# A fourth PSUM bank for the Gram products of a hybrid decoder layer, the upper rows of each inverse loaded first, and new orders for the last block and the drain

## The chip, the cores and the metric

The kernel runs on one core of one Trainium2 chip. The metric is the device time of one execution in microseconds (us); the figure for a kernel is the median of several executions. The engines are TensorE (PE in the profile; its weight loads are PEld), VectorE (DVE), ScalarE (ACT), GpSimd (POOL) and SyncE (SP, which here only issues DMAs). SBUF is the on-chip working memory, PSUM the eight banks into which TensorE writes.

## The reference, cut to what matters

One decoder layer on a sequence of 2048 tokens and a width of 1024. The part that the change touches is the RWKV-7 recurrence, which the kernel computes in chunks of 64 tokens, and the first steps of the SSD mixer behind it.

```python
def _rwkv7_scan(r, w, k, v, za, zb):          # 8 heads of 64
    def step(S, inp):
        r_t, w_t, k_t, v_t, a_t, b_t = inp
        sa = jnp.einsum("bhij,bhj->bhi", S, a_t)
        S = S * w_t[:, :, None, :] + sa[..., None] * b_t[:, :, None, :] + v_t[..., None] * k_t[:, :, None, :]
        return S, jnp.einsum("bhij,bhj->bhi", S, r_t)
    ...
def reference(x, ...):                          # DEPTH = 1
    xn = _rms_norm(h, pre_mix_norm[l])
    proj = (xn @ w_in[l]).astype(jnp.float32)
    p_ssd, p_rwkv = jnp.split(proj, [SSD_COLS], axis=-1)
    y_ssd = _ssd_mixer(p_ssd, ...)              # conv, softplus steps, chunked SSD, gate, norm
    y_rwkv = _rwkv7_mixer(p_rwkv, ...)          # token shift, low-rank decay, _rwkv7_scan, group norm, gate
    mix = jnp.concatenate([y_ssd, y_rwkv], axis=-1).astype(h.dtype) @ w_out[l]
    h = h + _rms_norm(mix, post_mix_norm[l])
    hn = _rms_norm(h, pre_ffn_norm[l])
    u = _causal_dwconv(hn @ ffn_w_up[l], ffn_conv_w[l], ffn_conv_b[l])
    gate, val = jnp.split(u, 2, axis=-1)
    f = (jax.nn.silu(gate) * val) @ ffn_w_down[l]
    h = h + _rms_norm(f, post_ffn_norm[l])
```

## The kernel before, in words

The program has three phases. The recurrence phase (`phase_R`, up to about 1005 us) works on 16 blocks of 128 tokens, two chunks of 64 each; `phase_S` does the SSD mixer and the output projection; `phase_F` the gated feed-forward part, which takes the second half of the span. Matrix products in float16 are done as three passes (high by high, high by low, low by high).

In the recurrence phase the order of TensorE's work is written out by hand: an iteration `it` runs through a list of step names, in which `f.` is block `it` (its front half), `b.` block `it - 1` (its back half), `a.` block `it - 2`, and `n.load` fetches the rows of block `it + 1`. FIRST is the list of iteration 0, SECOND of iteration 1, PLAN of iterations 2 to 14, LAST of iteration 15. DRAIN has only back steps; each `S` in it takes one step of the list S_DRAIN, the first work of the SSD phase. Only TensorE keeps the order of the lists. From iteration 1 on the order on VectorE, ScalarE, GpSimd and in SyncE's DMA queue is made at build time by a scheduler, which simulates the program and lets each engine take the instruction that is ready, earlier ones of the program first; each engine then keeps that order on the chip.

The front half of a block: `d.0` to `d.13` are projections of 24 matmuls each (L301), evicted in pairs by ScalarE (L439, L441) and mixed with the previous token by VectorE (L443); `low` is the low-rank decay, `scan` its running sum (L508) and two exponentials (L512, L513), `keys` and `norm` the normalised key (a square on ScalarE, L519, then the matmul `nq`, L527, a logarithm and an exponential, then BK on GpSimd and VectorE, L541 and L542). `conv.0` to `conv.7` are the projections of the SSD branch, with a causal convolution of taps (L464 on GpSimd, L469 and L474 on VectorE, stored by L475). `gram.0` and `gram.1` multiply BK with AR, per chunk and half of the heads one PSUM bank (`gr00`, `gr01`, `gr10`, `gr11`, L558), which VectorE masks into G (L562).

`solve` inverts the 64x64 triangular parts of G as 32x32 halves: SyncE writes them to DRAM (L574, two DMAs for each chunk) and reads them back one matrix per partition (`atl`, L578); a chain of 31 steps, each a product and a sum (L593, L596), does the substitution, on VectorE in every block but the last and on GpSimd there; the inverses go to DRAM (L601) and back into the tile XT (L607, four DMAs: for chunk `c` and half `b`, with `b` the inner loop). In the next iteration `merge.0` first transposes the upper half's inverse (XW, L641, one instruction on VectorE for each chunk, each of which needs the half `b = 0` of its chunk), then multiplies (`pw`, L648); `merge.1` (`po`, L652) completes the inverse. `own`, `update` and `state` are the products with the state of the recurrence, for chunk 0 and then chunk 1; `gate` and `finish` give the block's output (`finish.0` ends on GpSimd, L740; `finish.1` begins with transposes `yt` on TensorE, L745).

PSUM: the tag `ms` has 3 banks in rotation, used by `gr`, `nq`, `bt`, `vt`, `bo` and the low-rank products; `mm` has 2; `B` (merges, gate, `yt`), `U` and `Q` have one each. Eight are in use.

Of the kernel before, what the change touches and what calls it, by code (L numbers as in the profile page):

```python
# [209 lines left out]
f.chain.6 f.taps.5 f.chain.7 f.conv.7.0 f.taps.7  # L210
"""
SECOND = """
f.d.0 b.values f.d.1 f.d.2 f.d.3 f.d.4 f.low.0 b.own.0 f.low.1 f.scan f.d.5 f.keys f.d.6 f.d.7 f.d.8 b.merge.0 f.d.9
f.conv.0 f.conv.1 f.norm f.conv.2 f.conv.3 b.merge.1 f.receptance f.conv.4 b.update.0 f.gram.0 f.conv.5 f.gram.1
f.d.10 f.conv.6 f.conv.7 b.state.0 b.own.1 f.d.11 b.update.1 f.transposed.0 b.gate f.solve f.transposed.1 f.d.12
b.state.1 b.finish.0 f.d.13 n.load
"""
PLAN = """
f.d.0 f.d.1 b.values f.low.0 f.d.2 a.finish.1 f.d.3 f.d.4 f.low.1 f.scan f.d.5 f.d.6 f.d.7 b.own.0 f.d.8 f.conv.0 f.keys
f.d.9 f.conv.1 b.merge.0 f.norm f.conv.2 b.merge.1 f.conv.3 b.update.0 f.conv.4 f.receptance f.gram.0 f.gram.1 f.solve  # L220
n.load f.conv.5 f.conv.6 b.state.0 f.conv.7 b.own.1 f.transposed.0 f.d.10 f.d.11 b.update.1 f.d.12 b.state.1 b.gate
f.transposed.1 f.d.13 b.finish.0
"""
LAST = """
f.d.0 f.d.1 f.low.0 f.d.2 f.d.3 a.finish.1 f.d.4 f.d.5 f.low.1 f.scan b.values f.keys f.d.6 f.d.7 f.d.8 f.d.9 f.norm b.own.0
f.d.10 f.receptance f.d.11 b.merge.0 f.d.12 f.gram.0 b.merge.1 f.d.13 f.gram.1 f.solve b.update.0 f.conv.0 b.state.0
f.conv.1 b.own.1 f.conv.2 f.conv.3 b.update.1 f.transposed.0 f.conv.4 f.conv.5 b.state.1 f.transposed.1 f.conv.6
b.gate f.conv.7 b.finish.0
"""
DRAIN = """  # L230
S S b.values S S a.finish.1 S b.own.0 S S S S S S S S S S S S S S S S b.merge.0 S b.merge.1 S b.update.0 S b.state.0 S
b.own.1 S S b.update.1 S b.state.1 b.gate S b.finish.0 b.finish.1
"""


# [70 lines left out]
def phase_R(tc, K, const, tables, x, w_r, w_c, wl_d, g2_d, XN, XC, YR, filler, iters=16):  # L306
    nc = tc.nc
    V, S, G_ = nc.vector, nc.scalar, nc.gpsimd
    with ExitStack() as ctx:
# [56 lines left out]
        ub0 = (64, 0)  # L366
# [17 lines left out]
        def bank(name, tag, bufs=1):  # L384
            return psp.tile([P, 4, P], F32, name=name, tag=tag, bufs=bufs)

        class Block:
# [164 lines left out]
                        out=tr[:, j], in0=tr[:, j], scalar=K.p_r_k[:, j:j + 1], in1=tk[:, j], op0=ALU.mult, op1=ALU.mult)  # L552

            def gram(self, c):
                pg = [self.ms(f"gr{c}{hh}") for hh in range(2)]
                for j in range(4):
                    for hh in range(2):
                        nc.tensor.matmul(  # L558
                            pg[hh][:, j, :], self.BK[64 * hh:64 * hh + 64, j, c, :], self.AR[64 * hh:64 * hh + 64, j, c, :],
                            start=True, stop=True)  # L560
                for hh in range(2):
                    V.tensor_tensor(  # L562
                        out=self.G[:, c, hh], in0=pg[hh],
                        in1=K.gmask[:, c * P:(c + 1) * P].unsqueeze(1).to_broadcast([P, 4, P]), op=ALU.mult)
# [23 lines left out]
            def chain(self, part):  # L588
                atl, xl, tmp, XTd, it = self.atl, self.xl, self.tmp, self.XTd, self.it
                chain = G_ if it == iters - 1 else V  # L590
                for j in range(part * 4, min(part * 4 + 4, 31)):
                    n, m = 31 - j, j // 4 + 1
                    chain.tensor_tensor(  # L593
                        out=tmp[:, :m, :n], in0=atl[:, j, j + 1:32].unsqueeze(1).to_broadcast([P, m, n]),
                        in1=xl[:, :m, j:j + 1].to_broadcast([P, m, n]), op=ALU.mult)
                    chain.tensor_tensor(  # L596
                        out=xl[:, :m, j + 1:32], in0=xl[:, :m, j + 1:32], in1=tmp[:, :m, :n], op=ALU.add)
                if part < 7:
                    return
# [21 lines left out]
            def values(self):  # L621
# [148 lines left out]
        for it in range(iters + 1):  # L770
            if it == 1:
                begun.close()
            f = blocks[it] if it < iters else None
            b = blocks[it - 1] if it else None
# [10 lines left out]
            for step in (FIRST if b is None else SECOND if it == 1 else DRAIN if f is None else LAST if it == iters - 1 else PLAN).split():  # L785
# [10 lines left out]
                a = [int(v) for v in a]  # L796
# [1136 lines left out]
```

## Time and profile before

| | |
|---|---|
| median of 3 executions | 2626.78 us (2623.9 to 2636.14) |
| the profiled execution | 2628.14 us, of which the span from first to last instruction is 2626.4 us |
| TensorE busy | 2439.2 us, 93% of the span |
| VectorE, ScalarE, GpSimd busy | 75%, 46%, 50% |
| mean granted TensorE clock | 0.977 of full speed |
| iterations 2 to 14 | 173 to 874 us |
| iteration 15 (LAST) | 874 to 938 us |
| drain, to the last transposes | 938 to 1005 us |

All numbers of the trace are from this one profiled execution; times in it count from its first instruction. Columns and forms are explained with each group of rows.

### The profile page before, as it was taken

How to read it: one execution, taken by the hardware profiler on the slowest of the kernel's cores; microseconds unless marked ns; L12 is line 12 of the kernel's file. 1: busy time of each engine (PE TensorE's matmuls, PEld its weight loads, DVE VectorE, ACT ScalarE, POOL GpSimd, SP SyncE). 2: the span in 40 equal slices, each digit the busy share in tenths (PEclk: the TensorE clock that was granted, in tenths of full speed). 3: DMA queues.
4: the chain of work that ended last, by engine and by line, in shares of the span. 5: the costliest groups of instructions: out<-in, count | busy, mean ns of one | idle time of the engine just before them, and what ended most of it. 6: DMA issues, size and time to landing. Idle time of an engine off the chain costs nothing. (4 is left out here: it accounts for less than half of the span.)

```text
span 2626.4 us, 53869 instructions
## 1 busy us (share of the span) xinstructions
PE 2439.2 (93%) x21196; PEld 1536.1 (58%) x21212; DVE 1970.8 (75%) x3687; ACT 1211.5 (46%) x2467; POOL 1301.0 (50%) x1356
## 2 busy tenths in 40 slices
PE   5889999999999888999987999999989999999998
PEld 4788888888888855555543444444434444444443
DVE  6778777777877756677787979999999836455557
ACT  7455555555555444444544553534444433223132
POOL 2344444544444353445577675866757513223035
PEclk8899999999999999999998999999999999999999
DMA  7332222232222243556575444444436543333253
GB/s 219 72 70 67 54 61 57 64 86 54 54 64 56 48 170 121 158 162 177 154 209 184 167 147 154 142 171 168 149 128 204 168 143 102 103 96 106 87 156 109
DMA packets 344414, 319.14 MB, mean 122 GB/s; under 512 B 203232, under 2 KB 248672, under 8 KB 340832
## 3 DMA queue, kind: packets, MB, share of 16 engines
q1 hardware_dynamic: 342864, 314.12, 40.9%
q8 instruction: 166, 2.72, 0.5%
q10 hardware_dynamic: 1296, 1.58, 0.2%
q14 instruction: 88, 0.72, 0.1%
HBM read 187.85 MB, written 110.99 MB: 114 GB/s over the span
## 5 line engine op out<-in xcount | busy, mean ns | idle before, releaser
L1399 PE MATMUL u<-b,w 128*128 128x512 f16 x3696 | 811.2, 382 | 28.5 <-DVE C L1417 11.2
L1399 PEld LDWEIGHTS <-w 128*128 128x128 f16 x3696 | 363.1, 98 | 473.6 <-issue 38.8
L301 PE MATMUL d<-xt,wr 128*128 128x129 f16 x5376 | 337.8, 225 | 19.1 <-DMA xt<-xh 15.4
L301 PEld LDWEIGHTS <-wr 128*128 128x128 f16 x5376 | 323.2, 100 | 33.3 <-ACT wr L264 15.4
L1635 PE MATMUL d<-dw,fa 128*128 128x512 f16 x1512 | 333.7, 380 | 4.6 <-DVE dw L1599 2.3
L1635 PEld LDWEIGHTS <-fa 128*128 128x128 f16 x1596 | 157.1, 98 | 205.5 <-issue 19.1
L1417 DVE TENSOR_TENSOR C<-u,C 128x512 f32<-128x512 f32 x220 | 150.5, 684 | 156.3 <-PE u L1399 151.0
L301 PE MATMUL c<-xt,wc 128*128 128x131 f16 x3072 | 203.2, 225 | 18.7 <-ACT tr L441 9.6
L301 PEld LDWEIGHTS <-wc 128*128 128x128 f16 x3072 | 186.5, 99 | 35.3 <-issue 27.6
L1648 DVE TENSOR_TENSOR acc<-d,acc 128x512 f32<-128x512 f32 x212 | 140.1, 683 | 54.3 <-PE d L1635 53.4
L593 DVE TENSOR_TENSOR tmp<-atl,xl 128x60 f32<-128x60 f32 (+24 forms) x465 | 140.6, 302 | 41.5 <-DMA atl<-ATd 30.1
L1245 POOL TENSOR_TENSOR fa<-p,fa 128x512 f16<-128x512 f32 x100 | 142.1, 1434 | 40.1 <-ACT fa L1240 40.1
L1247 DVE SCALAR_TENSOR_TENSOR w<-us,w 128x512 f16<-128x512 f32 x132 | 144.5, 1105 | 17.4 <-ACT w L1240 16.4
L1452 DVE SCALAR_TENSOR_TENSOR p<-C,fpar,p 128x1024 f32<-128x1024 f32 x88 | 131.1, 1490 | 33.9 <-ACT p L1448 33.7
L469 DVE SCALAR_TENSOR_TENSOR ca<-rc,cw,ca 128x128 f32<-128x128 f32 x384 | 130.3, 385 | 24.8 <-POOL ca L464 24.5
L596 DVE TENSOR_TENSOR xl<-xl,tmp 128x60 f32<-128x60 f32 (+24 forms) x465 | 124.0, 267 | 11.3
L1452 DVE SCALAR_TENSOR_TENSOR a<-C,fpar,a 128x1024 f32<-128x1024 f32 x88 | 123.5, 1404 | 4.8 <-ACT a L1448 3.5
L1240 ACT ACTIVATE fa<-p 128x512 f16<-128x512 f32 x110 | 65.5, 623 | 131.9 <-DVE p L1465 120.0
L1371 POOL TENSOR_TENSOR us<-us,us 128x512 f32<-128x512 f32 x66 | 104.5, 1587 | 43.9 <-DVE w L1247 25.2
L706 POOL TENSOR_TENSOR tS<-S,Pi 64x256 f32<-64x256 f32 x64 | 41.4, 647 | 163.6 <-DVE S L716 161.2
L1458 POOL COPY fcarry<-C 128x2 f32<-128x2 f32 x88 | 40.5, 461 | 164.7 <-DVE C L1417 164.7
L1413 ACT ACTIVATE C<-u 128x512 f32<-128x512 f32 x88 | 52.0, 591 | 148.2 <-PE u L1399 128.5
(316 smaller groups left out, 4571.0 us busy)
## 6 DMA issues: line engine op xcount, KB each, us to landing
UW<-w SPq DMA_DIRECT2D x154, 256.0 KB
w<-UW SPq DMA_DIRECT2D x154, 256.0 KB
us<-in_w_u_dram SPq DMA_DIRECT2D x88, 256.0 KB
DW<-dw SPq DMA_DIRECT2D x70, 256.0 KB
dw<-DW SPq DMA_DIRECT2D x56, 256.0 KB
hs<-HN SPq DMA_DIRECT2D x48, 256.0 KB
r<-in_w_d_dram SPq DMA_DIRECT2D x10, 1024.0 KB
xin<-in_x_dram SPq DMA_DIRECT2D x16, 512.0 KB
```

Source lines behind the costliest of these rows:

```text
L301: nc.tensor.matmul(ps, w[:, a, kt, :], xt[:, b, kt, cols], start=n == 0, stop=n == 3 * KT - 1)
L469: V.scalar_tensor_tensor(out=acc[:, q], in0=raw[:, q, k:k + 128], scalar=cw[:, g + q, k:k + 1], in1=acc[:, q], op0=ALU.mult, op1=ALU.add)
L593: chain.tensor_tensor(out=tmp[:, :m, :n], in0=atl[:, j, j + 1:32].unsqueeze(1).to_broadcast([P, m, n]), in1=xl[:, :m, j:j + 1].to_broadcas ...
L596: chain.tensor_tensor(out=xl[:, :m, j + 1:32], in0=xl[:, :m, j + 1:32], in1=tmp[:, :m, :n], op=ALU.add)
L1245: {"V": V, "G": G_}[engine].tensor_tensor(out=l, in0=src, in1=h, op=ALU.subtract)
L1247: V.scalar_tensor_tensor(out=l, in0=src, scalar=scale, in1=h, op0=ALU.mult, op1=ALU.subtract)
L1371: op("G", 1.25, lambda: G_.tensor_tensor(out=st[o], in0=st[a], in1=st[b], op=alu), (n[a], n[b]), (n[o],))
L1399: nc.tensor.matmul(bk[at], self.w[i][:, u, k, :], self.half.b[i][:, k, v, :], start=start and n == 0, stop=n == 11, skip_group_check=True)
L1417: op("V", .61, lambda: V.tensor_tensor(out=part(j, x), in0=bk[at], in1=part(*a), op=ALU.add), (("u", 4 * s + at), (*(c0, c1)[a[0]], a[1])) ...
L1452: V.scalar_tensor_tensor(out=o[j], in0=C[j][:, 2 - d:1026 - d], scalar=cw[:, g, 2 - d:3 - d], in1=o[j], op0=ALU.mult, op1=ALU.add)
L1635: nc.tensor.matmul(bk[s, t], pairs[m].a[i][:, u, t * P:t * P + P], pairs[m].w[n][0][:, v, :], start=new and m == 0 and u == v == 0, stop=m ...
L1648: V.tensor_tensor(out=acc[j][:, t], in0=bk[s, t], in1=acc[j][:, t], op=ALU.add)
```

## The change

The Gram products of the second chunk's second half (`gr11`) get the bank of tag `B` in iterations 2 to 14 instead of one of `ms`. The four loads of XT run over `b` outside and `c` inside. The two transposes at the head of `merge.0` become a step of their own, `turn`, which every list has directly before `merge.0`. LAST, DRAIN and S_DRAIN are reordered: in LAST `low` and `norm` come earlier among the `d` steps, `own.0` comes behind `merge.0`, `gram.1` and `solve` stand around `d.13`; in DRAIN `own.0` comes earlier, `a.finish.1` later, `finish.0` ahead of two S steps; in S_DRAIN `t.steps` and `s.flip` come earlier, `c.keys` later.

```diff
 S_DRAIN = """
-s.steps c.z.0 c.z.1 c.z.2 c.z.3 s.sums n.z.0 s.flip c.rows n.z.1 n.z.2 n.z.3 c.begin m.z.0 c.off c.keys c.decay.0 m.z.1
-c.decay.1 m.z.2 m.z.3 t.steps u.z.0 u.z.1 u.z.2 n.rows c.y u.z.3 c.state
+s.steps c.z.0 c.z.1 c.z.2 c.z.3 s.sums s.flip n.z.0 c.rows n.z.1 n.z.2 n.z.3 c.begin m.z.0 t.steps c.off c.decay.0
+m.z.1 m.z.2 m.z.3 c.decay.1 u.z.0 c.keys u.z.1 n.rows c.y u.z.2 c.state u.z.3
 """
...
 LAST = """
-f.d.0 f.d.1 f.low.0 f.d.2 f.d.3 a.finish.1 f.d.4 f.d.5 f.low.1 f.scan b.values f.keys f.d.6 f.d.7 f.d.8 f.d.9 f.norm b.own.0
-f.d.10 f.receptance f.d.11 b.merge.0 f.d.12 f.gram.0 b.merge.1 f.d.13 f.gram.1 f.solve b.update.0 f.conv.0 b.state.0
-f.conv.1 b.own.1 f.conv.2 f.conv.3 b.update.1 f.transposed.0 f.conv.4 f.conv.5 b.state.1 f.transposed.1 f.conv.6
-b.gate f.conv.7 b.finish.0
+f.d.0 f.d.1 f.d.2 f.d.3 f.d.4 f.low.0 f.low.1 f.d.5 a.finish.1 f.scan b.values f.keys f.d.6 f.norm f.d.7 f.d.8 f.d.9
+f.receptance f.d.10 b.turn b.merge.0 f.d.11 b.own.0 f.gram.0 b.merge.1 f.d.12 f.gram.1 f.d.13 f.solve f.conv.0 b.update.0
+b.state.0 f.conv.1 b.own.1 f.conv.2 b.update.1 f.conv.3 b.state.1 f.conv.4 f.transposed.0 f.conv.5 f.conv.6
+f.transposed.1 b.gate f.conv.7 b.finish.0
 """
 DRAIN = """
-S S b.values S S a.finish.1 S b.own.0 S S S S S S S S S S S S S S S S b.merge.0 S b.merge.1 S b.update.0 S b.state.0 S
-b.own.1 S S b.update.1 S b.state.1 b.gate S b.finish.0 b.finish.1
+S S b.values b.own.0 S S S S S S S a.finish.1 S S S S S S S S S S S S b.turn b.merge.0 S b.merge.1 b.update.0 S
+b.state.0 S b.own.1 S S b.update.1 S b.state.1 b.gate b.finish.0 S S b.finish.1
 """
...
             def gram(self, c):
-                pg = [self.ms(f"gr{c}{hh}") for hh in range(2)]
+                side = c == 1 and 1 < self.it < iters - 1
+                pg = [self.ms(f"gr{c}0"), bank("gr11" + self.sf, "B") if side else self.ms(f"gr{c}1")]
...
-                for c in range(2):
-                    for b in range(2):
+                for b in range(2):
+                    for c in range(2):
                         r0 = ub0[c] + 32 * b
                         K.marks["solved"] = nc.sync.dma_start(
                             XT[r0:r0 + 32, :, 32 * b:32 * b + 32], XTd[c, b].rearrange("h x q i -> (x q) h i"))
...
+            def turn(self):
+                self.X11 = self.tl("XW", (8, 32))
+                for c in range(2):
+                    b0 = ub0[c]
+                    V.transpose(self.X11[b0:b0 + 32], self.XT[b0:b0 + 32, :, 0:32])
+
             def merge(self, step):
 
                 XT, Gv = self.XT, self.Gv
-                if step == 0:
-                    self.X11 = self.tl("XW", (8, 32))
-                    for c in range(2):
-                        b0 = ub0[c]
-                        V.transpose(self.X11[b0:b0 + 32], XT[b0:b0 + 32, :, 0:32])
                 X11 = Wm = self.X11
```

## Rows read from the trace of the kernel before

**Rows 1.** The page's part 1: engine, busy us, share, instructions.

```profile
PE 2439.2 (93%) x21196; PEld 1536.1 (58%) x21212; DVE 1970.8 (75%) x3687; ACT 1211.5 (46%) x2467; POOL 1301.0 (50%) x1356
```

**Rows 2.** TensorE's waits in iterations 2 to 14: waiter, releaser, total us, times, longest.

```profile
PE gr L558 <- DVE G L562: 17.8, 13, 1.4
PE pw L648 <- DVE XW L641: 9.1, 14, 1.9
```

**Rows 3.** TensorE's timeline, one turn: start, us, instruction, [idle before, releaser].

```profile
564.51 0.69 PE L648 MATMUL pw<-XW,G 32*32 32x32 f32 x30 [0.34 <-DVE XW L641]
...
572.58 1.38 PE L558 MATMUL gr<-AR,BK 64*128 64x128 f32 x18 [0.22 <-DVE BK L542]
575.41 1.16 PE L558 MATMUL gr<-AR,BK 64*128 64x128 f32 x14 [1.44 <-DVE G L562]
...
619.79 0.69 PE L648 MATMUL pw<-XW,G 32*32 32x32 f32 x30 [0.53 <-DVE XW L641]
```

**Rows 4.** VectorE's timeline in the same turn.

```profile
575.92 0.43 DVE L474 SCALAR_TENSOR_TENSOR ca<-ct,ca 128x256 f32<-128x256 f32 x1
576.39 1.29 DVE L562 TENSOR_TENSOR G<-gr,cst 128x512 f32<-128x512 f32 x2
...
586.44 0.19 DVE L593 TENSOR_TENSOR tmp<-atl,xl 128x31 f32<-128x31 f32 x1 [1.42 <-DMA atl<-ATd]
...
611.47 0.17 DVE L596 TENSOR_TENSOR xl<-xl,tmp 128x8 f32<-128x8 f32 x1
...
619.30 0.43 DVE L641 STREAM_TRANSPOSE XW<-XT 32x256 f32<-32x256 f32 x1 [0.34 <-DMA XT<-XTd]
```

**Rows 5.** SyncE's queue in that turn: start and us of the issues, line, DMA, count.

```profile
561.38 1.83 SPq L607 DMA_DIRECT2D XT<-XTd  x4
...
576.39 0.40 SPq L475 DMA_DIRECT2D XC<-ca  x1
...
577.41 1.28 SPq L411 DMA_TRANSPOSE xt<-xh  x1
578.79 1.03 SPq L574 DMA_DIRECT2D ATd<-G  x2
```

**Rows 6.** VectorE's waits for XT, iterations 2 to 14, and the longest, in its timeline.

```profile
DVE XW L641 <- DMA XT<-XTd: 24.1, 20, 2.5
...
508.53 0.43 DVE L641 STREAM_TRANSPOSE XW<-XT 32x256 f32<-32x256 f32 x1 [2.11 <-DMA XT<-XTd]
```

**Rows 7.** Iteration 15: TensorE and VectorE around `nq`; two other turns' scan and its input.

```profile
887.39 5.68 PE L301 MATMUL d<-xt,wr 128*128 128x129 f16 x96
898.64 2.08 PE L527 MATMUL nq<-sq,cst 128*128 128x512 f32 x2 [5.57 <-ACT sq L519]
...
890.71 0.47 DVE L596 TENSOR_TENSOR xl<-xl,tmp 128x8 f32<-128x8 f32 x1
...
892.07 2.17 DVE L508 TENSOR_TENSOR_SCAN Pv<-smask,thw 128x512 f32<-128x512 bf16 x1 [0.17 <-POOL thw L507]
...
556.75 1.22 DVE L508 TENSOR_TENSOR_SCAN Pv<-smask,thw 128x512 f32<-128x512 bf16 x1
...
606.72 1.50 POOL L507 TENSOR_SCALAR thw<-thw 128x512 f32<-128x512 f32 x1
```

**Rows 8.** A stretch behind `nq`: us, busy us (instructions) of PE, PEld, DVE, ACT, POOL, clock, DMA, GB/s.

```profile
898.60:908.60 10.00, 9.96 (x90) 8.18 (x90) 6.66 (x14) 3.97 (x7) 2.97 (x2) 0.57 0.16 41
```

**Rows 9.** TensorE's longest waits in the drain.

```profile
PE yt L745 <- POOL ysb L740: 5.7, 1, 5.7
PE z L957 <- DVE ws L265: 4.0, 2, 3.6
PE acs L922 <- DVE da L917: 2.2, 1, 2.2
```

**Rows 10.** The drain: GpSimd's work of `finish` inside the chain, and TensorE's `u.z.3`.

```profile
952.70 1.33 POOL L750 TENSOR_TENSOR yln<-yln,tv 128x512 f32<-128x512 f32 x1
...
992.92 1.47 PE L957 MATMUL z<-ws,xs 128*128 128x512 f16 x6
```

More of the change, by code (lines that the diff above doesn't have):

```diff
@@ L212 @@
 SECOND = """
-f.d.0 b.values f.d.1 f.d.2 f.d.3 f.d.4 f.low.0 b.own.0 f.low.1 f.scan f.d.5 f.keys f.d.6 f.d.7 f.d.8 b.merge.0 f.d.9
-f.conv.0 f.conv.1 f.norm f.conv.2 f.conv.3 b.merge.1 f.receptance f.conv.4 b.update.0 f.gram.0 f.conv.5 f.gram.1
+f.d.0 b.values f.d.1 f.d.2 f.d.3 f.d.4 f.low.0 b.own.0 f.low.1 f.scan f.d.5 f.keys f.d.6 f.d.7 f.d.8 b.turn b.merge.0
+f.d.9 f.conv.0 f.conv.1 f.norm f.conv.2 f.conv.3 b.merge.1 f.receptance f.conv.4 b.update.0 f.gram.0 f.conv.5 f.gram.1
 f.d.10 f.conv.6 f.conv.7 b.state.0 b.own.1 f.d.11 b.update.1 f.transposed.0 b.gate f.solve f.transposed.1 f.d.12
@@ L218 @@
 PLAN = """
[L219 to L222, printed above, removed]
+f.d.0 f.d.1 b.values f.low.0 f.d.2 a.finish.1 f.d.3 f.d.4 f.low.1 f.scan f.d.5 f.d.6 f.d.7 b.own.0 f.d.8 f.conv.0
+f.keys f.d.9 f.conv.1 b.turn b.merge.0 f.norm f.conv.2 b.merge.1 f.conv.3 b.update.0 f.conv.4 f.receptance f.gram.0
+f.gram.1 f.solve n.load f.conv.5 f.conv.6 b.state.0 f.conv.7 b.own.1 f.transposed.0 f.d.10 f.d.11 b.update.1 f.d.12
+b.state.1 b.gate f.transposed.1 f.d.13 b.finish.0
 """
 LAST = """
-f.d.0 f.d.1 f.low.0 f.d.2 f.d.3 a.finish.1 f.d.4 f.d.5 f.low.1 f.scan b.values f.keys f.d.6 f.d.7 f.d.8 f.d.9 f.norm b.own.0
-f.d.10 f.receptance f.d.11 b.merge.0 f.d.12 f.gram.0 b.merge.1 f.d.13 f.gram.1 f.solve b.update.0 f.conv.0 b.state.0
-f.conv.1 b.own.1 f.conv.2 f.conv.3 b.update.1 f.transposed.0 f.conv.4 f.conv.5 b.state.1 f.transposed.1 f.conv.6
-b.gate f.conv.7 b.finish.0
+f.d.0 f.d.1 f.d.2 f.d.3 f.d.4 f.low.0 f.low.1 f.d.5 a.finish.1 f.scan b.values f.keys f.d.6 f.norm f.d.7 f.d.8 f.d.9
+f.receptance f.d.10 b.turn b.merge.0 f.d.11 b.own.0 f.gram.0 b.merge.1 f.d.12 f.gram.1 f.d.13 f.solve f.conv.0 b.update.0
+b.state.0 f.conv.1 b.own.1 f.conv.2 b.update.1 f.conv.3 b.state.1 f.conv.4 f.transposed.0 f.conv.5 f.conv.6
+f.transposed.1 b.gate f.conv.7 b.finish.0
 """
 DRAIN = """
-S S b.values S S a.finish.1 S b.own.0 S S S S S S S S S S S S S S S S b.merge.0 S b.merge.1 S b.update.0 S b.state.0 S
-b.own.1 S S b.update.1 S b.state.1 b.gate S b.finish.0 b.finish.1
+S S b.values b.own.0 S S S S S S S a.finish.1 S S S S S S S S S S S S b.turn b.merge.0 S b.merge.1 b.update.0 S
+b.state.0 S b.own.1 S S b.update.1 S b.state.1 b.gate b.finish.0 S S b.finish.1
 """
```

## The prediction

> **What bounds the kernel now.** I read the busy shares first: TensorE is the fullest engine by far [rows 1], which suggests that every wait of TensorE that goes is time gained. Then TensorE's waits by releaser in iterations 2 to 14: the largest entry is the one that the fourth bank removes, 13 waits of `gr11` for the eviction of `gr00`, 17.8 us; beside it stand 14 waits for the transposed inverse XW, 9.1 us, at most 1.9 [rows 2]. So TensorE is nearly full, and yet it waits in nearly every iteration for the solve of the block before. To see which of the two sets the pace I followed one turn through the timelines of three engines, from one `merge.0` to the next [rows 3 to 5]. It takes 619.79 - 564.51 = 55.28 us: from `pw` to the first `gr` 8.07 (`nq` is queued right behind `pw`, and `gr` again waits a little, 0.22, for BK, which comes from `nq`); from there to the end of the second eviction pair, 576.39 + 1.29 = 577.68, 5.10; to the chain's first step 8.76, through SyncE's DMAs, with VectorE idle for the last 1.42; the chain runs from 586.44 to 611.64, 25.20; then come DMAs and two transposes, to 619.73. This is a closed loop: the solve of one block releases `merge.0` of the next iteration, and that releases the next solve. The 1.44 us wait of `gr11` lies beside it, not in it, except as far as it holds up the second eviction pair. The loop sets the pace; TensorE is some 0.7 us (9.1 / 13) ahead of it.
>
> **The fourth bank.** It removes 13 waits of about 1.4 us [rows 2, 3]. TensorE is then done with `gr` 1.44 earlier, at 575.1 instead of 576.57. What is late next is XW: arriving that much earlier at `merge.0`, TensorE waits there (or at the `c` before it, whose bank is freed behind the scan) that much longer, unless the loop gets shorter. VectorE evicts the second pair from 576.39, directly behind L474, which it ran from 575.92 while `gr11` was late [rows 4]. With the products there it can evict the second pair at once and run L474 after it: 0.44 us earlier, L474's time. SyncE's queue follows: the store L475 at 576.39 (0.40) needs L474 and stands ahead of the transposing DMA of 577.41 and of the second chunk's writes at 578.79 [rows 5]; if it goes behind the writes, these move up by about as much. I take 0.44 x 13 = 5.7 us. Low end: L474 and the transposing DMA stay where they are, the chain starts no sooner, 0. High end: the second chunk's writes also go ahead of the transposing DMA, as both are ready within half a microsecond; then they leave at 577.24 instead of 578.79, 1.55 a block, and the whole 17.8 us come through. The row nearest to the question is VectorE's, and it says 0.44. The new use of bank `B` makes `gr11` wait for the eviction of `po` and `gate` for that of `gr11`; in the list three steps and `gram.0` lie between the first two and a dozen steps between the others, so both cost nothing; without that cover it would be one eviction each, 0.4 to 0.7 (half of a pair of 1.29).
>
> **The upper rows first.** The second transpose of XW needs the third of four XT loads before, the second after. Four issues take 1.83 us, so one slot is 0.46 [rows 5]. VectorE waited 20 times for XT, 24.1 us in all: 12 times for the first transpose and 8 times more for the second, up to 2.11 us [rows 6]. Capping each of those 8 waits (0.23, 0.29, 0.34, 0.38, 0.39, 0.95, 1.28, 2.11) at one slot gives 3.0 us. Low end 0, high end their sum, 6.0. The lower rows come later but are needed only by `merge.1`, with `norm` and a `conv` between, so nothing is lost there. The wait of 2.11 shows a load that landed more than a slot behind its turn. The Trainium skill says why that may stay so (DMA: Bandwidth & Descriptors, Two DMAs through the same engine are not ordered): nothing orders the completion of DMAs across the 16 engines, whatever the order of issue. The trace agrees in that one place; by the rule alone this term would be 0 and the forecast 3 us higher. I keep 3.0, because most of the eight waits are of about a slot. `turn` as a step of its own changes no order: it stands directly before `merge.0` in every list.
>
> **LAST.** TensorE waited 5.57 us for the square ahead of `nq`, and in the 10 us behind it the granted clock was 0.57 of full, mostly the lower level of 1.2 GHz [rows 7, 8]: 10 x 0.43 = 4.3 us lost. After the change three `d` steps (5.68 / 4 = 1.42 each, 4.3) that lay before `nq` lie behind it. Whether that helps hangs on the square, which follows the scan on VectorE; the scan at 892.07 stood right behind the chain of block 14, which ended at 890.71 + 0.47 = 891.18. In another turn the scan's input was ready at 606.72 + 1.50 = 608.2, and the chain ran on to 611.64 before the scan [rows 4, 7]. If so here too, the scan begins 0.9 earlier at best, takes perhaps 1.22 as in a third turn instead of 2.17, and the square is 1.9 earlier: 4.3 - 1.9 = 2.4 lost. If the scan gets into the chain, TensorE is at `nq` at 887.39 + 1.42 and, allowing 1 for a wait at the earlier `low`, 889.8, waits for nothing, and 898.64 - 889.8 - 4.3 = 4.5 are gained, plus the slow clock's 4.3. Ends -2.4 and 8.8; nothing in the rows is nearer to one of them, so I take the middle, 3.2.
>
> **DRAIN and S_DRAIN.** TensorE's longest waits there are `yt` 5.7, `z` 4.0 and `acs` 2.2, 11.9 in all [rows 9]. One group `u.z.3`, 1.4 us [rows 10], goes into the wait before `yt`: 1.4 gained. `update.0` follows `merge.1` without a z group between, 1.4 less at the price of a wait of some 0.4 for XT (an estimate, the size of the gaps at `pw` [rows 3]): 1.0. `own.0` moves ahead of the `z` that waited and fills part of its 4.0; half of it, 2.0. `a.finish.1` issues three GpSimd instructions like that at 952.70 [rows 10] in the middle of the last chain, and one store on SyncE's queue; they move towards the chain's end, which I count at 0, and at up to 4 (three times 1.33) if the chain then ends that much sooner and TensorE is there. Sum 4.4. Low end -3: `own.0` now waits for the eviction of `vt`, and `acs` for an input from a VectorE that the earlier work finds just as full. High end 9, three quarters of the waits.
>
> **Sum.** 5.7 + 3.0 + 3.2 + 4.4 = 16.3 us off the profiled execution's 2628.1 (its span of 2626.4 and 1.7 around it) give 2611.8; the median shown lies 1.4 below that execution, so 2610.
>
> **Rivals.** *TensorE is the pace.* The loop gets 1.5 us shorter, by SyncE's order or by VectorE's work that now fits into its idle time ahead of the chain, and the bank's whole 17.8 come through with the other terms: 2628.1 - 28.4 - 1.4 = 2598. For it: 93% busy, and 1.42 idle ahead of the chain. Against: the waits for XW, which say that the loop is the longer one.
> *The wait only moves.* 0 from the bank, 3.0 from the loads, 2 at the end: 2622. For it: the loop, and the transposing DMA ahead of the writes. Its sign is in TensorE's waits for XW and at `c`, which grow by about 17.
> *Slower.* In LAST the square stays behind the chain and the `d` steps moved behind it run at the lower clock, as the matmuls of [rows 8] did: 4.3 us become 8.5, so 6.6 lost; the drain loses its 3, and at most 3 were gained before: 2628.1 + 6.6 + 3 - 3 - 1.4 = 2633. It decides once the wait at `nq` is longer than the 5.57 of before by the 1.9 that the square can gain or more. Against: the eviction of `d.13` no longer stands ahead of the last `gram.1`'s, so the last solve starts sooner.
>
> **Chances.** Forecast 0.45 (2603 to 2617), TensorE the pace 0.25, the wait only moves 0.22, slower 0.08. A measurement of this kernel can tell 0.5%, 13.1 us, from no change: below 2613.6 is faster, above 2639.9 slower. Faster: 0.45 x 0.77 + 0.25 = 0.60; slower 0.04, the far part of the last case; same 0.36. Range 2594 to 2624: it leaves out the best of the second case and the worst of the last two.
>
> **What would show it.** The waits of `gr` for G gone in 13 iterations. An iteration of 55.28 us shorter by 0.7 if the forecast holds, by 0.2 or 1.6 if the first two rivals do. Waits for XW and at `c` up by about 9 us in the forecast, by 17 if the wait only moves, down if TensorE is the pace. The second transpose directly behind the first. In iteration 15 the wait at `nq` and the clock behind it decide the third term; in the drain the wait before `yt` at about 4. The prediction is wrong if the chain's 25.20 us change, since no step of mine touches them, or if the SSD phase gives back what the recurrence gains: TensorE must stay as full there as it is.

## The result, and the profile after

Before: 2626.19 us, median of 5 runs (2619.76 to 2636.14). After: 2612.99 us, median of 5 (2609.58 to 2615.93). The ratio is 0.9949, 95% interval 0.9934 to 0.9964. In a second comparison beside other kernels it was 2617.98 against 2626.32, ratio 0.9964 (0.9947 to 0.9980). So 8 to 13 us are gained where 16.3 were forecast; both medians lie in the range given. The first comparison is just past 0.5%, the second just short of it.

The profiled execution took 2615.75 us. The page's part 1, in the form of [rows 1]:

```profile
PE 2438.8 (93%) x21212; PEld 1535.9 (59%) x21212; DVE 1968.8 (75%) x3687; ACT 1211.4 (46%) x2467; POOL 1310.1 (50%) x1356
```

The shares are those of before. TensorE's waits in twelve iterations do differ (waiter, releaser, total us, times, longest). Before (181 to 852 us), two entries that [rows 2] does not have:

```profile
PE c L301 <- ACT tr L441: 8.0, 10, 0.8
PE pS L711 <- ACT UV L694: 6.3, 6, 1.8
```

After (181 to 840 us):

```profile
PE pS L713 <- ACT UV L696: 16.1, 12, 2.2
PE c L301 <- ACT tr L441: 15.6, 10, 1.7
PE pw L650 <- DVE XW L639: 4.9, 11, 1.1
PE gr L559 <- DVE BK L542: 2.2, 10, 0.2
```

The waits of `gr` for G are gone. But `pS`, the product in `state.1` for which I had no row, waits 16.1 us where it waited 6.3 before, and `c` 15.6 where it was 8.0. In sum TensorE waited 42.2 us in these twelve iterations before and 39.1 after.

One turn of TensorE, as in [rows 3]:

```profile
558.32 0.85 PE L650 MATMUL pw<-XW,G 32*32 32x32 f32 x32
566.55 2.06 PE L559 MATMUL gr<-AR,BK 64*128 64x128 f32 x32 [0.21 <-DVE BK L542]
584.05 0.69 PE L713 MATMUL pS<-UV,BT 128*64 128x64 f32 x16 [1.43 <-ACT UV L696]
608.61 1.56 PE L301 MATMUL c<-xt,wc 128*128 128x131 f16 x24 [1.73 <-ACT tr L441]
613.38 0.24 PE L650 MATMUL pw<-XW,G 32*32 32x32 f32 x2 [0.44 <-DVE XW L639]
```

VectorE in the same turn, as in [rows 4]:

```profile
557.53 0.90 DVE L639 STREAM_TRANSPOSE XW<-XT 32x256 f32<-32x256 f32 x2 [1.08 <-DMA XT<-XTd]
568.63 1.28 DVE L563 TENSOR_TENSOR G<-gr,cst 128x512 f32<-128x512 f32 x2
569.89 0.43 DVE L474 SCALAR_TENSOR_TENSOR ca<-ct,ca 128x256 f32<-128x256 f32 x1
570.23 1.28 DVE L563 TENSOR_TENSOR G<-gr,cst 128x512 f32<-128x512 f32 x2
575.36 3.04 DVE L469 SCALAR_TENSOR_TENSOR ca<-rc,cw,ca 128x128 f32<-128x128 f32 x7 [2.33 <-POOL ca L464]
581.13 0.19 DVE L594 TENSOR_TENSOR tmp<-atl,xl 128x31 f32<-128x31 f32 x1 [1.51 <-DMA atl<-ATd]
605.79 0.17 DVE L597 TENSOR_TENSOR xl<-xl,tmp 128x8 f32<-128x8 f32 x1
```

The two transposes of XW stand together, in one row; over the twelve turns the second waited for its load by itself once, before eight times. L474 still lies between the two eviction pairs. And SyncE, as in [rows 5]:

```profile
570.35 0.40 SPq L475 DMA_DIRECT2D XC<-ca  x1
570.80 0.47 SPq L575 DMA_DIRECT2D ATd<-G  x1
571.37 1.29 SPq L411 DMA_TRANSPOSE xt<-xh  x1
572.77 1.01 SPq L575 DMA_DIRECT2D ATd<-G  x2
```

The store and the transposing DMA still stand ahead of the second chunk's writes. So G is ready a little sooner, and SyncE's queue takes it back. The table gives means over the twelve turns from the first `gr` of iteration 2 to that of iteration 14, in us after that `gr` or as lengths, worked out from the trace of each run (the step between the chain's end and the first XT issue, 4.1 to 4.5 everywhere, is left out), and TensorE's summed waits behind the first of these `gr` and up to the last (a listing of waits can have one wait more or less, as its window is in round numbers):

| kernel | G done | chain starts | chain | XT issue to XW end | XW end to next `gr` | iteration | waits |
|---|---|---|---|---|---|---|---|
| before | 5.13 | 14.52 | 25.21 | 3.77 | 8.24 | 55.91 | 42.2 |
| after, first trace | 4.90 | 14.50 | 24.92 | 3.37 | 8.24 | 55.15 | 39.1 |
| after, second trace (r_after) | 4.95 | 14.57 | 25.11 | 3.41 | 8.12 | 55.50 | 36.9 |
| a1_bank | 4.90 | 14.48 | 25.07 | 3.74 | 8.24 | 55.71 | 43.4 |
| a2_loads | 5.01 | 14.43 | 25.21 | 3.34 | 8.25 | 55.42 | 38.1 |
| a3_bank_loads | 4.91 | 14.25 | 24.93 | 3.45 | 8.23 | 55.01 | 38.4 |
| a5_old_last | 4.95 | 14.63 | 25.16 | 3.30 | 8.13 | 55.46 | 39.4 |
| b2_after_pace | 4.93 | 12.85 | 25.76 | 3.14 | 9.14 | 55.13 | 39.3 |
| d1_gate | 4.91 | 14.55 | 24.83 | 3.26 | 8.24 | 55.05 | 37.4 |
| d2_gate_pace | 4.96 | 12.88 | 25.87 | 3.10 | 9.11 | 55.24 | 38.8 |
| h1_norm_sdt | 8.53 | 15.46 | 25.91 | 3.03 | 8.67 | 57.56 | 53.4 |
| h2_taps_sdt | 4.96 | 12.63 | 25.19 | 3.01 | 9.62 | 54.78 | 36.7 |
| i4_order | 7.64 | 14.81 | 25.59 | 2.96 | 8.35 | 56.19 | 35.3 |
| i6_early_wo | 4.95 | 12.55 | 25.17 | 3.04 | 8.13 | 53.17 | 16.9 |

How far one trace can be trusted shows in a3 and a5: they run the same instructions in this stretch, and differ by 0.45 an iteration, 5 us in all.

Iteration 15, TensorE, as in [rows 7]:

```profile
881.99 2.08 PE L527 MATMUL nq<-sq,cst 128*128 128x512 f32 x2 [3.43 <-ACT sq L519]
901.53 1.40 PE L559 MATMUL gr<-AR,BK 64*128 64x128 f32 x14 [3.16 <-DVE G L563]
```

The wait at `nq` fell from 5.57 to 3.43; in the 10 us from the start of `nq` the granted clock is 0.84, where [rows 8] has 0.57. A wait of 3.16 stands at `gram.1` that was not there. VectorE had evicted `gram.0` late because it stood behind this:

```profile
900.10 0.23 DVE L848 TENSOR_TENSOR sdt<-sdt,par 128x64 f32<-128x64 f32 x1 [3.43 <-DMA sdt<-in_w_dt_dram]
```

In the second trace of the same kernel TensorE's wait is nearly absent (846.8 to 928.8 us), but VectorE's is not:

```profile
PE gr L559 <- DVE G L563: 0.2, 1, 0.2
```

```profile
903.17 0.23 DVE L848 TENSOR_TENSOR sdt<-sdt,par 128x64 f32<-128x64 f32 x1 [2.61 <-DMA sdt<-in_w_dt_dram]
```

So the size of TensorE's wait belongs to the execution, and its cause to the new order: in all five traces with the new LAST and without the `sdt` edit of h1, VectorE waits 2.2 to 3.4 us for this small weight ahead of the evictions of `gram.0`, and TensorE then 0 to 3.16 us at `gram.1`. In the five traces with the old LAST VectorE never waits for it. The drain's waits (927.3 to 993.1 us), against [rows 9]:

```profile
PE yt L747 <- POOL ysb L742: 3.2, 1, 3.2
PE pq L678 <- ACT UV L629: 2.7, 1, 2.7
PE bc L1004 <- DVE dv L906: 2.5, 1, 2.5
PE pu L693 <- ACT qs L686: 1.4, 1, 1.4
```

`yt` waits less, and `own.0` (`pq`), `bc` and `pu` wait where they had not. From `yt` to the end the two traces take 1622.6 us before and 1622.0 after: the later phases gave nothing back.

### The profile page after: what moved, and what is told of

The parts are those of the page before. It is cut to its first block, busy times and chain, and to the rows that moved or that the text cites. A ratio compares the mean times of both kernels' runs of the same rounds, so it can differ in the third digit from the quotient of the medians.

```text
span 2614.0 us, 53918 instructions
## 1 busy us (share of the span) xinstructions
PE 2438.8 (93%) x21212; PEld 1535.9 (59%) x21212; DVE 1968.8 (75%) x3687; ACT 1211.4 (46%) x2467; POOL 1310.1 (50%) x1356
## 5 line engine op out<-in xcount | busy, mean ns | idle before, releaser
L301 PE MATMUL d<-xt,wr 128*128 128x129 f16 x5376 | 342.1, 226 | 18.5 <-DMA xt<-xh 14.8
L301 PE MATMUL c<-xt,wc 128*128 128x131 f16 x3072 | 201.3, 224 | 26.3 <-ACT tr L441 17.3
L469 DVE SCALAR_TENSOR_TENSOR ca<-rc,cw,ca 128x128 f32<-128x128 f32 x384 | 130.7, 384 | 46.5 <-POOL ca L464 45.4
L1249 DVE SCALAR_TENSOR_TENSOR w<-us,w 128x512 f16<-128x512 f32 x132 | 143.4, 1097 | 16.1 <-ACT w L1242 15.1
L597 DVE TENSOR_TENSOR xl<-xl,tmp 128x60 f32<-128x60 f32 (+24 forms) x465 | 140.7, 303 | 12.2
L594 DVE TENSOR_TENSOR tmp<-atl,xl 128x60 f32<-128x60 f32 (+24 forms) x465 | 121.7, 262 | 36.6 <-DMA atl<-ATd 24.7
L1242 ACT ACTIVATE w<-us 128x512 f16<-128x512 f32 x132 | 80.6, 624 | 80.7 <-POOL us L1373 44.2
```

Source lines behind the costliest of these rows:

```text
L301: nc.tensor.matmul(ps, w[:, a, kt, :], xt[:, b, kt, cols], start=n == 0, stop=n == 3 * KT - 1)
L469: V.scalar_tensor_tensor(out=acc[:, q], in0=raw[:, q, k:k + 128], scalar=cw[:, g + q, k:k + 1], in1=acc[:, q], op0=ALU.mult, op1=ALU.add)
L594: chain.tensor_tensor(out=tmp[:, :m, :n], in0=atl[:, j, j + 1:32].unsqueeze(1).to_broadcast([P, m, n]), in1=xl[:, :m, j:j + 1].to_broadcas ...
L597: chain.tensor_tensor(out=xl[:, :m, j + 1:32], in0=xl[:, :m, j + 1:32], in1=tmp[:, :m, :n], op=ALU.add)
L1242: S.activation(h, src, AF.Copy, **({} if scale is None else {"scale": scale}))
L1249: V.scalar_tensor_tensor(out=l, in0=src, scalar=scale, in1=h, op0=ALU.mult, op1=ALU.subtract)
```

## The experiments

**Parts of the change.** a1: the kernel before with the bank alone.

```diff
-pg = [self.ms(f"gr{c}{hh}") for hh in range(2)]
+side = c == 1 and 1 < self.it < iters - 1
+pg = [self.ms(f"gr{c}0"), bank("gr11" + self.sf, "B") if side else self.ms(f"gr{c}1")]
```

> The kernel before with the fourth Gram bank alone. Theory, two causes: the bank shortens the closed solve loop only because TensorE, 1.4 us ahead, lets VectorE finish the conv taps before the solve's chain starts, so the chain falls from 25.2 to 24.9 us, while the stretch from the first XT load's issue to the end of the second XW transpose stays at 3.77; iteration 55.91 to 55.6, some 4 us in all, about 2622. Rival, one cause: the chain is shorter only because XW comes earlier through the loads; then the bank alone gives nothing, iteration 55.9, about 2626, and the waits of gr for G reappear whole before pw. Second rival, the bank is the whole gain: iteration 55.15, about 2615.

Measured: 2624.17 against 2626.74, ratio 0.9988 (0.9976 to 1.0000). TensorE's waits, 181 to 848 us:

```profile
PE pS L712 <- ACT UV L695: 15.9, 12, 2.3
PE c L301 <- ACT tr L441: 15.7, 10, 1.7
PE pw L649 <- DVE XW L642: 9.3, 14, 1.9
```

The 16.4 us of `gr` came back as 7.7 at `c` and 9.6 at `pS`; the sum is 43.4, where it was 42.2. By its interval the time alone does not rule out the rival's nothing. In the trace the iteration got 0.2 shorter, with a chain of 25.07: between its steps VectorE has 3 conv taps of L469 in each turn, 1.0 us, where it had 6, 2.1 us.

a2: the load order alone.

```diff
-for c in range(2):
-    for b in range(2):
+for b in range(2):
+    for c in range(2):
```

> The kernel before with the other order of the XT loads alone. Theory, two causes: from the first XT load's issue to the end of the second XW transpose 3.4 us instead of 3.77, the chain stays at 25.2, the waits of gr for G stay; iteration 55.91 to 55.5, some 5 us in all, about 2621. Rival, one cause: everything comes from the loads, chain 24.9 too, iteration 55.15, about 2615. Second rival: TensorE with its waits of gr is then the pace and the loads alone give nothing: about 2626.

Measured: 2620.11, ratio 0.9978 (0.9965 to 0.9992), 6 us, with the waits of `gr` for G still there (181 to 845 us):

```profile
PE gr L558 <- DVE G L562: 16.2, 12, 1.5
PE c L301 <- ACT tr L441: 9.0, 11, 0.8
PE pw L648 <- DVE XW L641: 4.7, 10, 1.1
```

From the first XT issue XW is ready 0.43 sooner, the chain stays at 25.21, and the waits at `pw` are halved. The theory of two causes holds in the traces, with more weight on the loads than on the bank.

a3: both edits, the lists of before for iteration 15, drain and first SSD steps.

> The bank and the load order together, with the lists of before for iteration 15, the drain and the first SSD steps. Theory, two causes, and lists that gave little: iteration 55.15, the first gram of iteration 14 some 10.8 us earlier than before, as in the kernel after, and iteration 15 and the drain as long as before: about 2615. Rival, the lists carry what was forecast for them (7.6): about 2621.

Measured: 2620.61, ratio 0.9972 (0.9959 to 0.9986), 7.4 us. That is the rival's number, 2621, but the trace has the theory's iteration, 55.01, and the first `gr` of iteration 14 at 841.0 instead of 852.7. The profiled execution, 2616.54, is one of the faster of twelve (2612.19 to 2623.52).

a5: the kernel after with the old list of iteration 15 (`LAST` of before, `b.turn` put in ahead of `b.merge.0`).

> The kernel after with iteration 15's list of before; the new drain and first SSD steps stay. Theory, the new list of iteration 15 gains nothing (its shorter wait at nq is paid back by gram.1's 3.16 us wait for VectorE, which stood behind a small weight's DMA): iteration 15 lasts 64.4 us as before, TensorE waits 5.6 at nq and not at gram.1, total within 2 us of the kernel after, about 2613 to 2614. Rival, the list of iteration 15 gains and the drain loses: 2 to 5 us slower than the kernel after. Second rival, the new list loses and the drain gains: some 3 us faster.

Measured: 2620.73, ratio 0.9973 (0.9961 to 0.9986), no better than a3, and by the ratios 2 to 6 us behind the kernel after. This speaks against the theory: the list of iteration 15 carries some of the gain, and the new drain none that can be measured. The intervals overlap, so the times alone do not show it; the traces do. From the first `gr` of iteration 14 to the drain's first step the five traces with the old list take 85.0 to 86.6 us; the kernel after takes 85.3 with the wait of 3.16 and 82.1 without it, and b2, d1 and d2 below, with the same list, 79.8 to 83.2.

The kernel after once more, beside the next three:

> The kernel after once more, beside the next three, and to be held against the kernel with bank and loads alone (2620.6 in its own comparison). Theory, the new lists of iteration 15 and the drain are worth little: 2613 to 2619, no more than 3 of the 13 us from the lists. Rival, the lists carry some 7 of the 13 us: 2611 to 2615, with iteration 15 and the drain 6 to 8 us shorter in the trace than in the kernel with bank and loads alone.

Measured: 2617.98, ratio 0.9964, as told above. Against a3 the lists are worth 2 to 6 us by the two ratios.

**What sets the pace.** b2: the next block's transposing DMAs go behind the reads of `atl` on SyncE. (`pace` keeps an instruction behind a marked one in its engine's order.)

```diff
+turned = [nc.sync.dma_start_transpose(xt[:, a, :, 16:144], v) for a, v in enumerate((hi, lo))]
+if it > 1:
+    for d in turned:
+        pace(tc, K, d, "atl")
```

> The kernel after with the two transposing DMAs of the next block's load queued on SyncE behind the four reads of atl, instead of between the writes of ATd. Theory, the closed solve loop is the pace: atl is read some 1.2 us sooner, the chain starts 13.2 us after the first gram instead of 14.5, and the iteration falls from 55.15 by 0.6 to 1.2 us until TensorE's waits for XW (0.4 an iteration) and at c behind the scan (1.3) are used up: 2598 to 2606 if the kernel after is at 2613. Rival, TensorE's own list is the pace: its waits at c and pS have other causes, the chain starts sooner and the iteration stays at 55.1: about 2613. Second rival: with the chain sooner the conv taps are late behind it, pS waits grow by as much: 2610 to 2613.

Measured: 2610.68, ratio 0.9931 (0.9913 to 0.9949). The chain starts 1.7 us sooner, and the iteration is only 0.37 shorter than in the second trace of the kernel after: the chain has taken in conv taps (25.76; 3.3 us of them in each turn, where the kernel after has 1.5), and behind XW 1.0 is lost. TensorE's waits, 181 to 839 us:

```profile
PE gr L562 <- DVE BK L545: 12.0, 10, 1.2
PE pu L696 <- ACT qs L689: 10.3, 9, 2.4
PE pS L716 <- ACT UV L699: 6.5, 10, 0.8
```

The earlier chain came as the theory had it, the shorter iteration did not. The time is the second rival's, and so are the late taps, but the waits grew at `gr` for BK and at `pu`, and at `pS` they shrank: the loop has another side, from the scan to BK.

d1: `gate` ahead of `state.1`.

```diff
-f.d.12 b.state.1 b.gate f.transposed.1
+f.d.12 b.gate b.state.1 f.transposed.1
```

> The kernel after with gate (1.2 us of TensorE) ahead of state.1 instead of behind it in the steady list, so that the wait of state.1's pS for UV, 1.34 us an iteration, has work beside it. Theory, the solve loop is the pace: the waits of pS go from 16 us to about 3 and come back for XW at pw and at c, the iteration stays at 55.15, within 2 us of the kernel after. Rival, TensorE is the pace: 1.1 us an iteration gained, some 13 us, about 2600.

Measured: 2611.25, ratio 0.9941 (0.9924 to 0.9958), which overlaps that of the kernel after. The waits of `pS` fell to 5.9, those at `c` rose to 17.7, and `vt` waits 6.8: in sum 37.4 against 36.9. In the trace filling the wait only moved it. The medians are 6.7 us apart, more than the theory's 2 and half of the rival's 13, so a small gain is not excluded.

d2: both.

> Both edits together: transposing DMAs behind the reads of atl, and gate ahead of state.1. Theory, the solve loop is the pace and TensorE close behind it: with the loop shorter by 1.3 us TensorE's waits decide, so gate, worth nothing alone, now adds to the first edit: iteration 53.9, 2596 to 2600, 2 to 8 us under the first edit alone. Rival, TensorE is the pace: the gain of gate alone and no more. Second rival: neither is the pace alone, each gives its half.

Measured: 2608.44, ratio 0.9928 (0.9910 to 0.9946), iteration 55.24: `gate` adds nothing to the first edit that the intervals could tell. The theory, by which the two add up to 53.9, fell; TensorE's order is not the pace by itself.

h1: on top of b2, `norm` and the grams earlier in TensorE's list, and VectorE's multiply of `sdt` ordered behind the last gram's evictions.

```diff
-f.d.9 f.conv.1 b.turn b.merge.0 f.norm f.conv.2 ... f.conv.4 f.receptance f.gram.0 f.gram.1 f.solve
+f.d.9 f.norm f.conv.1 b.turn b.merge.0 f.conv.2 ... f.receptance f.gram.0 f.gram.1 f.solve f.conv.4
+pace(tc, K, d, "gram")   # d: sdt's multiply; "gram": the last G eviction
```

> Two edits on top of the paced transposing DMAs. First, in the steady list norm (the square's matmul nq) goes two steps up, ahead of conv.1 and merge.0, and the two gram steps go ahead of conv.4. Theory, the solve loop closes only through the order of TensorE's list, XW to pw to nq to BK to gr: from the end of XW to the next gr 9.1 us become some 7, the 13 us of gr's waits for BK go, iteration 55.1 to 53.5, about 2595. Rival, the second path from the chain's end (scan, keys, square, nq, BK) through VectorE and ScalarE is as long: gr still waits for BK, or XW's transposes stand behind more of VectorE's work, and the iteration stays at 55: about 2610. Second, in iteration 15 and the drain, VectorE's multiply of the small weight sdt is ordered behind gram.1's evictions. Theory, TensorE's wait at gram.1 (3.16 in the kernel after) goes and the stretch from the first gram of iteration 14 to the drain's first step falls from 86 by 2 to 3 us. Rival, the wait turns up behind it, at pS or own, and the stretch stays.

Measured: 2634.98 against 2623.77, ratio 1.0045 (1.0031 to 1.0058), slower. `gr` still waits for BK, 22.1 us, and G is done 8.53 after the first `gr` instead of 4.9. VectorE has two conv taps between the two eviction pairs, and they last 1.84 and 2.00 us instead of 0.34 each, in every turn, beside two instructions of GpSimd (the last section has more on this):

```profile
639.78 3.75 DVE L472 SCALAR_TENSOR_TENSOR ca<-rc,cw,ca 128x128 f32<-128x128 f32 x2
639.34 2.13 POOL L292 TENSOR_TENSOR xin<-xin,xh 128x1024 f16<-128x1024 f32 x1 [1.32 <-DVE ca L472]
```

From XW's end to `gr` it takes 8.67, not the theory's 7: the order of TensorE's list alone does not close the loop. The `sdt` edit did its part: VectorE waits nowhere for this weight any more, and TensorE not at `gram.1`, here and in h2.

h2: on top of b2, the first tap operation of conv groups 4 to 7 on ScalarE, and the `sdt` edit.

```diff
+if i > 0 and g > 3:
+    S.activation(acc[:, q], raw[:, q, 3:131], AF.Identity, scale=cw[:, g + q, 3:4], bias=cb[:, g + q:g + q + 1])
+    continue
 G_.tensor_scalar(
```

> On top of the paced transposing DMAs: the first of the four conv tap operations of the conv groups 4 to 7 on ScalarE instead of GpSimd, and the same later place of sdt. Theory, the chain is 25.8 us long there because conv taps, late through GpSimd (VectorE idle 2.33 us for them ahead of the chain), are worked between its steps; with the taps earlier the chain falls to 24.9 to 25.2, the waits of pu and pS for ScalarE shrink, and the iteration falls by 0.5 to 54.6: about 2604. Rival, what the chain gains is lost behind it on the path from the scan to BK: gr's waits grow, the iteration stays at 55.1, about 2610. Second rival, ScalarE, in whose order the four operations now stand ahead of other evictions, holds TensorE up: slower than 2611. The sdt place is worth 2 to 3 us in iteration 15 as in the run beside it.

Measured: 2610.12, ratio 0.9940 (0.9924 to 0.9956). The chain is back at 25.19, and much of what it gained is lost behind it: 9.62 from XW to `gr`, with 20.4 us of waits for BK. The iteration is 0.35 shorter than in b2, the time is the rival's. VectorE there:

```profile
553.95 0.43 DVE L646 STREAM_TRANSPOSE XW<-XT 32x256 f32<-32x256 f32 x1 [5.01 <-DMA XT<-XTd]
561.10 0.68 DVE L537 SCALAR_TENSOR_TENSOR kkn<-sq,kkn 128x512 f32<-128x512 f32 x1
```

and ScalarE's result for `kkn`:

```profile
558.91 0.63 ACT L536 ACTIVATE sq<-sq 128x512 f32<-128x512 f32 x1
```

The input of `kkn` was there at 559.54, and VectorE came to it 1.56 later, working off what had queued behind the XW transposes while it idled 5.01 for XT.

i4: h2, with `tk`'s multiply moved to `keys` and XW's transposes ordered behind it, and the four `r_k` multiplies behind BK.

```diff
+K.marks["tk"] = V.tensor_tensor(out=tk, in0=tk, in1=tm, op=ALU.mult)   # in keys, not in norm
+d = V.transpose(self.X11[b0:b0 + 32], self.XT[b0:b0 + 32, :, 0:32])
+pace(tc, K, d, "tk" if self.it < iters - 1 else "dv")
+pace(tc, K, d, "bk")   # each r_k multiply
```

> The kernel with paced transposing DMAs, four tap operations on ScalarE and the later sdt, and on top of it VectorE's order between the chain's end and BK. There VectorE idled 4.8 us an iteration for XT with tk's multiply and two tr operations queued behind the XW transposes, and did them, four r_k multiplies and conv taps ahead of kkn, whose operands were there 1.6 us before. Edit: tk's multiply moves from norm to keys, the transposes of XW are ordered behind it (in the drain behind dv of the second SSD steps), and the r_k multiplies behind BK. Theory, after the scan VectorE's in-order work up to BK is the second side of the solve loop: gr's waits for BK (20.4 us) fall below 5, from XW's end to the next gr 9.6 us become 8.2 to 8.5, the iteration 54.8 to 53.6, and the drain's 8.2 us wait at bc for dv falls below 3: 2586 to 2596. Rival, GpSimd's 1.84 us square times Pv between kkn and BK, and ScalarE's exponentials ahead of it, set BK: gr's waits stay above 12, about 2605. Second rival, the transposes of XW are now late and pw waits: 2610 or more.

Measured: 2625.13 against 2623.26, ratio 1.0007 (0.9992 to 1.0023). The theory's sign is there (no wait of `gr` for BK is left), and the time is not: the `r_k` multiplies now stand ahead of the G evictions, G is done at 7.64, and the wait went to `pS`, 26.3 us. The first eviction pair is only 0.6 later for it. Most of the rest is the tap between the pairs, which in every turn falls beside GpSimd's `xin` and lasts 2.15 instead of 0.43:

```profile
580.67 2.15 DVE L481 SCALAR_TENSOR_TENSOR ca<-ct,ca 128x256 f32<-128x256 f32 x1 [0.34 <-ACT ct L480]
580.41 2.14 POOL L292 TENSOR_TENSOR xin<-xin,xh 128x1024 f16<-128x1024 f32 x1 [2.35 <-DVE G L571]
```

TensorE's summed waits are 35.3 against 36.7 in h2, but it also worked slower. TensorE and then the windows (us, busy us and instructions by engine, clock, DMA share, GB/s) around one such wait:

```profile
595.36 0.69 PE L722 MATMUL pS<-UV,BT 128*64 128x64 f32 x16 [2.09 <-ACT UV L705]
597.17 2.07 PE L738 MATMUL zg<-GL,g 128*128 128x128 f32 x8
```

```profile
590.70:595.36 4.66, 2.57 (x42) 2.32 (x41) 4.03 (x20) 1.67 (x5) 0.00 (x0) 1.00 0.70 152
595.36:600.00 4.64, 4.64 (x46) 4.39 (x46) 4.24 (x18) 1.82 (x3) 0.66 (x1) 0.66 0.85 215
```

Ahead of the wait the granted clock was 1.00, behind it 0.66, so for some two thirds of the 4.64 us the lower level of 1.2 GHz; `zg` took 2.07, where the kernel before has 1.16 at 996.00. Over the twelve iterations the clock is 0.95 and TensorE works 638.8 us, against 1.00 and 619.9 in h2.

i6: the same without the `r_k` order, and VectorE's half of the `wo` split ordered behind `dv` in the drain.

```diff
-pace(tc, K, d, "bk")
-split_w(tc, WO[:, 0, kt, :], WO[:, 1, kt, :], ...)
+pace(tc, K, split_w(tc, WO[:, 0, kt, :], WO[:, 1, kt, :], ...), "dv")   # split_w now returns VectorE's half
```

> As the run before, but the r_k multiplies stay where they were, ahead of kkn, where VectorE then idled 1.25 us an iteration for ScalarE's exponential; behind BK they had pushed the G evictions from 5.0 to 7.6 us after the first gram. And VectorE's half of the wo weight split is ordered behind dv in the drain, where dv stood behind it and TensorE waited 8.9 us at bc. Theory, VectorE's order is the second side of the solve loop: G ends 5.0 after the first gram again, the chain starts at 12.6, from XW's end to the next gr stays at 8.4 to 8.7, iteration 53.6 to 54.0 instead of 56.2, pS waits small again, no lowered clock behind them; the wait at bc below 3: 2588 to 2598. Rival, what r_k takes ahead of kkn is paid there in full, gr waits for BK come back (above 12 us): iteration 54.8, about 2604. Second rival, pS's waits stay above 20 us with the lower clock behind them: 2615 or more.

Measured: 2593.34 against 2625.31, ratio 0.9878 (0.9857 to 0.9898). This beats both kernels, by 32 us the one before and by some 20 the one after. The iteration is 1.61 shorter than in h2, 19 us in twelve, which covers the 16 us between the two ratios; no run has one of the two edits that are left without the other. TensorE's waits, 181 to 820 us:

```profile
PE pq L690 <- DVE S L726: 7.6, 12, 0.6
PE pS L721 <- ACT UV L704: 3.7, 5, 1.1
PE pw L658 <- DVE XW L646: 3.0, 9, 0.8
PE gr L566 <- DVE BK L549: 2.6, 12, 0.2
```

VectorE, one turn:

```profile
548.00 0.43 DVE L646 STREAM_TRANSPOSE XW<-XT 32x256 f32<-32x256 f32 x1 [0.22 <-DMA XT<-XTd]
552.93 0.69 DVE L542 SCALAR_TENSOR_TENSOR kkn<-sq,kkn 128x512 f32<-128x512 f32 x1 [0.61 <-ACT sq L541]
```

`kkn` now waits for its input, 0.61, instead of the input for it. The iteration is 53.17, and TensorE works for 51.7 of it, at a clock of 1.00. In the drain the wait at `bc` for `dv` is gone; a wait of 4.4 for a DMA stands there in its place.

## Why the prediction was right, and where not

**The loop.** That a closed loop through the solve sets the pace, and TensorE's waits move round it, held in the traces: a1 and d1 each took a wait away, and it stood elsewhere. But I drew the loop through SyncE, XW and `nq`, with the chain as a constant, and said that the prediction was wrong if the chain's 25.20 changed. It did: 24.92 and 25.11 in the two traces. By that sign this part of the mechanism was wrong, though the number came near. b2, h2 and i6 show what I had left out: VectorE's work in its order is a side of the loop too. b2 started the chain 1.7 sooner and got 0.37 an iteration; h2 to i6 took work from between XW and BK and got 1.61.

**The bank, 5.7.** Alone it gave 3.2 (0 to 6.3) by time, which does not rule out 5.7, and 2.4 in the trace (0.20 in each of twelve iterations), and not by the step I wrote: L474 did not go behind the second pair. The 0.23 that G gained was lost on SyncE: the chain starts at 14.48, before at 14.52. What it gave came through the chain, where fewer conv taps were left to be done between its steps. I expected the moved wait at `pw` and `c`, about 9 us; with the whole change `c` rose by 7.6, `pw` fell by 4.2, and `pS`, which I had not named, rose by 9.8. Why the wait goes to `pS` no run here settles.

**The loads, 3.0.** Too small by the trace: I capped each of eight waits at one slot of 0.46. In a2 XW was ready 0.43 sooner on average, 5.2 us in twelve iterations, near the sum of 6.0 that I had as the high end. By time a2 gave 5.8 (2 to 9), which does not rule out 3.0. The Trainium skill (DMA: Bandwidth & Descriptors, Two DMAs through the same engine are not ordered) would have let this term be 0. Nothing in this kernel makes the loads land in the order of their issue, and yet in the two traces of the kernel after VectorE waited for the second load by itself in one and three of twelve iterations, where it did in eight before (13 and 15 waits for XT in all, before 20).

**LAST, 3.2.** Between -2.4 and 8.8 I took the middle. The condition of the high end came true, as the scan got into the chain (876.70, with the chain until 881.75), but not all that I drew from it: `nq` waits for 3.43, not for nothing. The clock in the 10 us from `nq` was 0.57 to 0.69 in the five traces with the old list and is 0.84 and 0.69 in the two of the kernel after, 0.83 or 0.84 in the seven other runs with the new one. The stretches above say 0 to 4 us in these two, less where the wait behind `sdt`, which I had not seen, struck.

**DRAIN and S_DRAIN, 4.4: the step that failed.** TensorE's waits there fell by about what I said, from 14.0 to 18.5 in the four traces with the old lists to 11.6 to 12.8 in four with the new ones (a5, both of the kernel after, d1); b2 and d2, whose edits lie ahead of the drain, have 16.9 and 9.4. The time did not fall: from the drain's first step to `yt` it took 61 to 66 us with the old lists and 61 to 69 in these six. For the same work, 463 matmuls, TensorE was busy from 47.1 us (a2, clock 0.93) to 56.8 (a5, clock 0.80). My step from 4.4 us of waits to 4.4 us of time left the clock out; in a stage with a clock of that spread it does not hold. Whether the new order itself lowers the clock stays open. The low end I had named, `own.0` waiting for `vt`'s eviction, came true with 2.7.

So it is luck that the sum came as near as it did, 8 to 13 us for 16.3: in it stand errors of opposite sign, the loads too small by the trace, the bank and the drain too large.

## What to carry to other kernels

Where every wait removed comes back elsewhere, follow the closed loop engine by engine, and read the in-order queue of the engine in it that looks idle: its idle time in front of a late transfer is worth filling with what now stands behind that transfer. Check what a reordered instruction is put in front of, and beside, as h1 and i4 show. And settle a gain of under 0.5% by parts and by repeated runs, not by one trace.

## What the hardware showed

VectorE's L474 takes 0.43 us at 569.89 of the trace after and 1.49 at 564.40, where GpSimd runs this beside it:

```profile
563.77 1.84 POOL L541 TENSOR_TENSOR sq<-kkn,Pv 128x512 f32<-128x512 f32 x1 [3.30 <-PE c L301]
```

It ends at 565.89, just after GpSimd's 565.61. The Trainium skill (SBUF — State Buffer, Who interferes with whom) says that a VectorE instruction with two SBUF inputs contends with a GpSimd instruction that reads SBUF, over a port pair that only one of them holds at a time. The trace agrees, with 1.06 us lost here. Which of the two pays changes from turn to turn: in eight of the twelve turns L538 of VectorE takes its 0.69, GpSimd's instruction 1.84 and then L474 1.49; in the other four GpSimd's takes 1.27 and L538 1.78. In h1 and i4 the same thing fell between the G evictions and held up the solve. It does not take every long instruction of GpSimd: beside one of 1.66 us on 8 columns (`gnr`, 526.79 in i6) VectorE's multiplies of `tv` keep their 0.34.
